# Expert products from raw 4-byte weights, with a branch on the token count

## The chip, the cores and the metric

One core of a Trainium2 chip runs the whole program. The metric is the device time of one execution in microseconds (us). Five engines work side by side: PE (TensorE: matrix products and, apart, the loads of their stationary operand), VectorE (DVE), ScalarE (ACT), GpSimd (POOL) and SyncE (SP, which issues most transfers). Products go to PSUM; operands lie in SBUF; DMA queues move data between SBUF and memory.

## The reference

One layer of a hybrid decoder on 1024 tokens of width 1024 in 4-byte floats: a modulated norm, one wide input projection, a recurrent branch, a sparse attention branch, a gated merge, and a mixture of 32 experts, of which each token uses two. Only the experts change:

```
xs = xf[row_tok].reshape(n_blk, MOE_BLOCK, D_)         # tokens of one expert, 128 to a block
hid = jax.nn.silu(xb @ w1[e]) * (xb @ w3[e])           # [128,1024] x [1024,512], twice
ys = hid @ w2[e]                                       # [128,512] x [512,1024]
out = segment_sum(ys * row_gate[:, None], row_tok)     # back to the tokens, then h += g2 * out
```

Counted from the reference's inputs, the 32 experts get 22 to 102 tokens: 17 of them at most 64, 11 from 65 to 96, 4 from 97 to 128, and none more.

## The kernel before

Everything up to the routing (the projections, attention, merge, output projection and the router's logits, in `project_out`) stays as it is but for a few lines at its end, where the lists of tokens and gates per expert are made. Then `experts` (L1395) runs over the 32 experts.

An expert has 128 slots, of which its tokens fill the first. Its weights, 6.29 MB, come as six transfers of 1 MB into a ring of 13 SBUF buffers (`ring_tile`, `prefetch`, `raw_load`: 8 buffers in `ring_a`, 5 in `ring_b`, which go back after expert 18). The transfers stand on SP's queue in the order in which they are used; each waits until its buffer is free.

PE multiplies in a rounded 4-byte format (`F32R`) in which each operand is the sum of a high and a low part. `weights` (L1464) splits each raw half buffer: ACT copies it to a rounded high part (L1472), VectorE subtracts that to get the low part (L1474). A product of two split operands is three products: high by high, high by low, low by high.

`expert` (L1458) is a generator that does one expert in steps:

- eight transposes on PE turn the 128 gathered token rows `xg` into `ptx` (L1483); ACT and VectorE split them into `xh` and `xl`;
- first products (L1501): the tokens stand still, 512 columns of w1 or w3 move; two sums `pa` and `pb` in PSUM over 8 blocks of 128 inputs, three products for each, so 48 in all;
- `hid` = silu(`pa`) x `pb` (L1506, L1507), four transposes into `pth` (L1483), and their split into `hh` and `hl`;
- last products (L137 to L139, `mm3`): `hid` stands still, 512 columns of w2 move; two sums `py`, 24 products;
- VectorE scales `py` by the gates and by the layer's gate row into `ye` (L1539), and POOL adds `ye` to the tokens' rows in memory by an indirect transfer (L1543). POOL also gathers the tokens of the expert that comes two later (L1453).

The loop in `experts` interleaves the steps, so that PE does the last products of expert e-1 beside the first of e and the transposes of e+1; within that, a scheduler sets the order on each engine. A branch (L1618) after expert 18 skips a loop for experts of more than 128 tokens, which these inputs don't need. The last two experts are not scattered: `combine` adds them by products with one-hot rows, makes the final norm and writes the output. Of what stands here, the change touches these functions:

Of the kernel before, what the change touches and what calls it, by code (L numbers as in the profile page):

```python
# [37 lines left out]
X_TAGS = [("xh", D), ("xl", D), ("hid", DE), ("hh", DE), ("hl", DE), ("ye", D)]  # L38
AHEAD = 3
NL = 4  # L40
RM = 4
RA, RB = 4 + RM, 5
NW = 6
RU = [-1, -1, -1, -1, -1, -1, -1, 6] + [3, 3, 4, 4, 4]
# [37 lines left out]
class Trunk:  # L82
# [866 lines left out]
    def merge(self, keep, ph):  # L949
# [21 lines left out]
        self.ring, self.uses = list(range(RA + RB)), list(RU)  # L971
# [164 lines left out]
    def project_out(self):  # L1136
# [5 lines left out]
        self.gate_l = hp.tile([P, NE], F32, name="gate_l")  # L1142
# [6 lines left out]
        with ExitStack() as st:  # L1149
# [128 lines left out]
            nc.scalar.activation(self.gate_l, R["gates"], AF.Copy)  # L1278
# [79 lines left out]
    def expert_weights(self, e, w1, w3, w2):  # L1358

        v1, v3 = (w.rearrange("(p k) f -> p (k f)", k=KT) for w in (w1, w3))  # L1360
        v2 = w2.rearrange("(p k) f -> p (k f)", k=4)
        h = [slice(0, 2048), slice(2048, 4096)]
        return [(v[:, h[c]], f"{n}_{e}_{c}") for c in range(2) for v, n in ((v1, "w1"), (v3, "w3"))] + [
            (v2[:, h[c]], f"w2_{e}_{c}") for c in range(2)
        ]

    def ring_tile(self, name, dt=F32):

        self.seq += 1
        i = self.ring.pop(0)  # L1370
        self.uses[i] -= 1
        if self.uses[i]:
            self.ring.append(i)
        pool, tag = (self.ring_a, f"ra{i}") if i < RA else (self.ring_b, f"rb{i - RA}")
        return pool.tile([P, 2048], dt, name=name, tag=tag)
# [19 lines left out]
    def experts(self):  # L1395

        nc, io = self.nc, self.io
        with ExitStack() as st:
# [4 lines left out]
            xp.tile([P, 640], F32, name="pad_at", tag="pad")  # L1403
            mp = self.pool(st, "moe")
            tp = self.pool(st, "moeps", bufs=2, space=PSUM)
            for n, b in (("whi", NW), ("wlo", NL)):
                mp.tile([P, D], F32R, name=f"{n}_at", tag=n, bufs=b)
# [6 lines left out]
            self.prefetch(RA + RB - self.seq)  # L1414
# [11 lines left out]
            def start(e):  # L1426
# [3 lines left out]
                if e < NE:  # L1430
                    gens[e] = self.expert(
                        xp, mp, tp, e, xgs[e % NXG], self.idx[:, e : e + 1], self.gate_l[:, e : e + 1],
                        [self.next_raw] * 6, NW, scatter=e < NE - 2,
                    )
                    step(e)
# [3 lines left out]
            for e in range(NE + 1):  # L1439
                step(e)  # L1440
                step(e - 1)
                step(e)
                start(e + 1)
                step(e - 1)
                if e == OV:

                    assert max(self.ring) < RA
                    rst.close()
                    self.overflow(xp, tp)
            self.combine(xp, mp, tp)  # L1450
# [7 lines left out]
    def expert(self, xp, mp, tp, e, xg, idx, gate, raws, nw, scatter=True):  # L1458
        nc = self.nc
        T = lambda n, e, shape, dt=F32: xp.tile(list(shape), dt, name=f"{n}_{e}", tag=n, bufs=2)  # L1460
        W = lambda n, e: mp.tile([P, D], F32R, name=f"{n}_{e}", tag=n, bufs=nw)
        raws = iter(raws)

        def weights(name):  # L1464
            raw = next(raws)()
            for g in range(2):
                hi, part = W("whi", f"{name}{g}"), raw[:, g * D : (g + 1) * D]
                lo = mp.tile([P, D], F32R, name=f"wlo_{name}{g}", tag="wlo", bufs=min(nw, NL))
                early = e == 0 and name[-1] == "0" and name[0] != "2"
                eng = nc.gpsimd if e == 0 and name[0] == "1" and name[-1] == "0" else nc.vector  # L1470
                with self.tc.issue_after(self.rooted) if early else nullcontext():
                    self.last_hi = nc.scalar.activation(hi, part, AF.Copy).ins  # L1472
                with self.tc.issue_after(self.listed) if early else nullcontext():
                    eng.tensor_tensor(lo, part, hi.bitcast(F32), op=OP.subtract)  # L1474
                yield hi, lo

        def tr(dst_h, dst_l, src, n, name):

            v = src.rearrange("t (p k) -> t k p", k=n)
            for g in range(0, n, 4):  # L1480
                pt = tp.tile([P, 4, P], F32, name=f"pt{name}_{e}_{g}", tag="pt")
                for k in range(4):
                    nc.tensor.transpose(pt[:, k, :], v[:, g + k, :], self.ident)  # L1483
                self.hilo(dst_h[:, g : g + 4, :], dst_l[:, g : g + 4, :], pt)

        xh, xl = T("xh", e, (P, KT, P), F32R), T("xl", e, (P, KT, P), F32R)
        tr(xh, xl, xg, KT, "x")
        yield
        pa = self.mmp.tile([P, 512], F32, name=f"pa_{e}", tag="mm")
        pb = self.mmp.tile([P, 512], F32, name=f"pb_{e}", tag="mm")  # L1490
        for c in range(2):
            if c:
                yield
            for ps, nm in ((pa, "1"), (pb, "3")):
                for g, (hi, lo) in enumerate(weights(f"{nm}_{e}_{c}")):

                    for b, As in ((hi, (xh, xl)), (lo, (xh,))):
                        for k in range(2):
                            kk = 4 * c + 2 * g + k
                            for a in As:  # L1500
                                nc.tensor.matmul(  # L1501
                                    ps, a[:, kk, :], b[:, k * DE : (k + 1) * DE], start=kk == 0 and a is xh and b is hi,
                                    stop=kk == KT - 1 and b is lo,
                                )
        hid = T("hid", e, (P, DE))
        nc.scalar.activation(hid, pa, AF.Silu)  # L1506
        nc.vector.tensor_tensor(hid, pb, hid, op=OP.mult)  # L1507
        yield
        hh, hl = T("hh", e, (P, 4, P), F32R), T("hl", e, (P, 4, P), F32R)
        tr(hh, hl, hid, 4, "h")  # L1510
        yield
        final = e == NE - 1
        pool, tag = (self.mmp, "mm") if final else (tp, "py")
        py = [pool.tile([P, 512], F32, name=f"py_{e}_{f}", tag=tag) for f in range(2)]

        def second(kk, f, hi, lo):
            s_ = slice(f * 512, (f + 1) * 512)
            self.mm3(py[f], hh[:, kk, :], hl[:, kk, :], hi[:, s_], lo[:, s_], kk == 0, kk == 3)

        for c in range(2):  # L1520
            w = weights(f"2_{e}_{c}")
            if final and c:
                w = list(w)
                for f in range(2):
                    for k in range(2):
                        second(2 + k, f, *w[k])
                continue
# [185 lines left out]
```

## Time and profile before

| | us |
|---|---|
| median of 3 runs (1865.74 to 1870.61) | 1866.28 |
| the profiled execution | 1865.06 |
| its span, first to last instruction | 1863.3 |
| PE busy | 1759.3 |
| VectorE busy | 1439.9 |
| ACT busy | 1170.1 |

The profile records every instruction with its start and a duration. Matmuls overlap: a matmul's duration covers filling and draining, so the time that PE spends on one is read from start to start. PEld is PE's loading of stationary operands, which overlaps PE. The granted clock is a share of 2.4 GHz: 1.00, or 0.50 for 1.2 GHz. "Idle before" is the time an engine stood still ahead of an instruction, with what ended it. Lines such as L1501 are lines of the kernel before.

### The profile page before, as it was taken

How to read it: one execution, taken by the hardware profiler on the slowest of the kernel's cores; microseconds unless marked ns; L12 is line 12 of the kernel's file. 1: busy time of each engine (PE TensorE's matmuls, PEld its weight loads, DVE VectorE, ACT ScalarE, POOL GpSimd, SP SyncE). 2: the span in 40 equal slices, each digit the busy share in tenths (PEclk: the TensorE clock that was granted, in tenths of full speed). 3: DMA queues.
4: the chain of work that ended last, by engine and by line, in shares of the span. 5: the costliest groups of instructions: out<-in, count | busy, mean ns of one | idle time of the engine just before them, and what ended most of it. 6: DMA issues, size and time to landing. Idle time of an engine off the chain costs nothing. (4 is left out here: it accounts for less than half of the span.)

```text
span 1863.3 us, 24597 instructions
## 1 busy us (share of the span) xinstructions
PE 1759.3 (94%) x8532; PEld 1456.1 (78%) x8532; DVE 1439.9 (77%) x2393; ACT 1170.1 (63%) x1730; POOL 398.8 (21%) x249
## 2 busy tenths in 40 slices
PE   3999999997999999999999999979999999999995
PEld 2788877786777888999788877858888888788774
DVE  6688876697777766778524456569999999999998
ACT  6565677725676767888512113348888887777765
POOL 4101002210010001212000001033554544344134
PEclk9999999998999999999999999979999999999998
DMA  9213754322112212121738544369989999999994
GB/s 297 61 35 104 237 179 147 109 89 65 59 54 73 68 58 93 55 66 57 216 107 252 194 152 170 138 238 350 379 329 344 363 376 367 366 380 371 357 338 182
DMA packets 163738, 366.85 MB, mean 197 GB/s; under 512 B 17855, under 2 KB 107543, under 8 KB 139160
## 3 DMA queue, kind: packets, MB, share of 16 engines
q1 hardware_dynamic: 152112, 340.50, 51.3%
q0 software_dynamic: 10192, 19.99, 3.9%
q10 hardware_dynamic: 1304, 4.74, 0.6%
q8 instruction: 68, 1.11, 0.3%
q14 instruction: 62, 0.51, 0.1%
HBM read 326.90 MB, written 54.53 MB: 205 GB/s over the span
## 5 line engine op out<-in xcount | busy, mean ns | idle before, releaser
L1472 ACT ACTIVATE whi<-raw_w 128x1024 fp32r<-128x1024 f32 x384 | 395.6, 1057 | 107.8 <-DMA raw_w<-in_moe_w_dram 28.2
L1474 DVE TENSOR_TENSOR wlo<-raw_w,whi 128x1024 fp32r<-128x1024 f32 x382 | 447.9, 1220 | 13.1 <-ACT whi L1472 4.7
L139 PE MATMUL pj<-uhi,wlo_in 128*128 128x512 f32 (+2 forms) x784 | 302.8, 387 | 5.6 <-POOL wlo_in L128 4.2
L137 PE MATMUL pj<-uhi,whi_in 128*128 128x512 f32 (+2 forms) x784 | 304.3, 388 | 1.2 <-ACT gq L706 1.2
L138 PE MATMUL pj<-ulo,whi_in 128*128 128x512 f32 (+2 forms) x784 | 302.0, 385 | 0.0
L1543 POOL DMA_INDIRECT h_spill<-ye,idx x30 | 179.4, 5980 | 215.0 <-DVE ye L1539 202.2
L139 PEld LDWEIGHTS pj<-uhi,wlo_in 128*128 128x128 f32 (+1 forms) x784 | 146.4, 187 | 37.8 <-POOL wlo_in L128 6.4
L137 PEld LDWEIGHTS pj<-uhi,whi_in 128*128 128x128 f32 (+1 forms) x784 | 146.6, 187 | 32.1 <-ACT gq L706 2.4
L138 PEld LDWEIGHTS pj<-ulo,whi_in 128*128 128x128 f32 (+1 forms) x784 | 146.6, 187 | 29.9 <-issue 1.0
L654 ACT ACTIVATE junk_a<-B,nt 128x768 bf16<-128x768 f32 (+2 forms) x93 | 96.8, 1041 | 49.6 <-DVE nt L650 41.2
L1501 PE MATMUL pa<-whi,xh 128*128 128x512 f32 x256 | 103.3, 403 | 0.6 <-ACT xh L97 0.5
L138 PE MATMUL py<-wlo,hh 128*128 128x512 f32 x256 | 100.9, 394 | 2.7 <-DVE wlo L1474 2.7
L1501 PE MATMUL pa<-whi,xl 128*128 128x512 f32 x256 | 100.6, 393 | 0.5 <-DVE xl L98 0.5
L137 PE MATMUL py<-gh,whi_y 128*128 128x512 f32 x256 | 99.9, 395 | 1.1 <-ACT gh L97 1.1
L1501 PE MATMUL pb<-whi,xh 128*128 128x512 f32 x256 | 100.0, 391 | 0.4 <-ACTq L1618 0.4
L139 PE MATMUL py<-gh,wlo_y 128*128 128x512 f32 x256 | 100.4, 393 | 0.0
L138 PE MATMUL py<-gl,whi_y 128*128 128x512 f32 x256 | 100.2, 393 | 0.1
L139 PE MATMUL py<-whi,hl 128*128 128x512 f32 x256 | 100.0, 391 | 0.0
L137 PE MATMUL py<-whi,hh 128*128 128x512 f32 x256 | 99.8, 400 | 0.1
L1501 PE MATMUL pb<-whi,xl 128*128 128x512 f32 x256 | 99.7, 389 | 0.0
L128 POOL TENSOR_TENSOR wlo_in<-raw_in,whi_in 128x1024 fp32r<-128x1024 f32 (+1 forms) x20 | 50.3, 2515 | 230.4 <-ACT whi_in L127 230.4
L127 ACT ACTIVATE whi_y<-raw_y 128x1024 fp32r<-128x1024 f32 x16 | 17.0, 1062 | 104.5 <-PE py L138 98.6
(403 smaller groups left out, 4119.2 us busy)
## 6 DMA issues: line engine op xcount, KB each, us to landing
raw_w<-in_moe_w_dram SPq DMA_DIRECT2D x191, 1024.0 KB, 12.6
raw_in<-in_w_in_dram SPq DMA_DIRECT2D x50, 512.0 KB, 3.5
wm<-in_w_mod_dram SPq DMA_DIRECT2D x32, 512.0 KB, 4.7
sg_spill<-gq SPq DMA_DIRECT2D x16, 512.0 KB, 2.6
sg<-sg_spill SPq DMA_DIRECT2D x32, 256.0 KB, 3.2
wm<-in_w_mod_dram SPq DMA_DIRECT2D x24, 256.0 KB, 5.8
g_spill<-ge SPq DMA_DIRECT2D x10, 512.0 KB, 2.6
gr<-g_spill SPq DMA_DIRECT2D x10, 512.0 KB, 3.6
```

What stands on the lines that cost most here:

```text
L127: nc.scalar.activation(hi[:, :n], raw[:, :n], AF.Copy)
L128: eng.tensor_tensor(lo[:, :n], raw[:, :n], hi[:, :n].bitcast(F32), op=OP.subtract)
L137: mm(ps, ah, bh, start=start, stop=False)
L138: mm(ps, ah, bl, start=False, stop=False)
L139: mm(ps, al, bh, start=False, stop=stop)
L654: nc.scalar.activation(junk_a[:, :n], self.B[j], AF.Sign, bias=nt[:, i : i + 1], accum_out=cnt[:, i : i + 1])
L1472: self.last_hi = nc.scalar.activation(hi, part, AF.Copy).ins
L1474: eng.tensor_tensor(lo, part, hi.bitcast(F32), op=OP.subtract)
L1501: nc.tensor.matmul(ps, a[:, kk, :], b[:, k * DE : (k + 1) * DE], start=kk == 0 and a is xh and b is hi, stop=kk == KT - 1 and b is lo,)
L1543: nc.gpsimd.indirect_dma_start(out=self.hd, out_offset=bass.IndirectOffsetOnAxis(ap=idx, axis=0), in_=ye, in_offset=None, bounds_check=S - ...
```

## The change

The weights are no longer split. In the first products the raw weights stand still, in blocks of 128 inputs by 128 hidden columns (every fourth column, so that the result is already turned for the last products), and the turned tokens move: 64, 96 or 128 slots, by the expert's count. PE reads the count into a register and branches; the other engines work on all 128 slots. Both sums take one PSUM bank each, `ph[0]` and `ph[1]`, and `hT` = silu(`ph[0]`) x `ph[1]` needs no transpose. In the last products 64 slots of `hT` stand still and 512 columns of the raw w2 move; the two halves of the output columns go to partitions 0 to 63 and 64 to 127 of one bank, `py[0]` for slots 0 to 63 and `py[1]` for the others, which is left out where the count is at most 64. All of these products are in plain 4-byte floats. The buffers of the split parts are gone; the ring gets 4 more (17 up to expert 18, 12 after it). PE's order is the one in which the loop writes it: `ptx` of e+1, last products of e-1, first products of e+1. The six transfers of an expert come in the order w1, w1, w3, w3, w2, w2.

```diff
-RA, RB = 4 + RM, 5
-NW = 6
+RA, RB, RC = 4 + RM, 5, 4
+RU = [-1] * RA + [5] * RB + [-1] * RC
...
+            nc.vector.tensor_copy(self.n_e, pn[:, :NE])
...
-            nc.scalar.activation(self.gate_l, R["gates"], AF.Copy)
+            for g in range(2):
+                self.both(self.gate_h[g], R["gates"][g * 64 : (g + 1) * 64, :])
...
+            self.ph = [tp.tile([P, 4, P], F32, name=f"ph_{i}") for i in range(2)]
+            self.py = [tp.tile([P, 512], F32, name=f"py_{i}") for i in range(2)]
...
+            for t in self.ph + self.py:
+                nc.vector.memset(t, 0.0)
...
-            for e in range(NE + 1):
-                step(e)
-                step(e - 1)
-                step(e)
-                start(e + 1)
-                step(e - 1)
+            for e0, e1 in ((0, OV + 1), (OV + 1, NE + 1)):
+                with self.as_traced((mybir.EngineType.PE,)):
+                    for e in range(e0, e1):
+                        step(e)
+                        start(e + 1)
+                        step(e - 1)
+                        step(e - 1)
...
+            n = nc.values_load(
+                count, engines=[mybir.EngineType.PE], min_val=0, max_val=S,
+            )
+        xT = T("xT", e, (P, KT, P))
...
+                nc.tensor.transpose(pt[:, k, :], v[:, g + k, :], self.ident)
+            nc.scalar.activation(xT[:, g : g + 4, :], pt, AF.Copy)
...
+        def first(m):
+            for ps, cs in zip(self.ph, w):
+                for b in range(4):
+                    for k in range(KT):
+                        blk = cs[k // 4][:, (k % 4) * DE : (k % 4 + 1) * DE].rearrange("p (f b) -> p b f", b=4)
+                        nc.tensor.matmul(
+                            ps[:, b, :m], blk[:, b, :], xT[:, k, :m], start=k == 0, stop=k == KT - 1
+                        )
...
+            with tc.If(n > 64) as more:
+                with tc.If(n > 96) as most:
+                    first(P)
+                with most.Else():
+                    first(96)
+            with more.Else():
+                first(64)
+        hid, hT = T("hid", e, (P, 4, P)), T("hT", e, (P, 4, P))
+        self.last_act = nc.scalar.activation(hid, self.ph[0], AF.Silu).ins
+        nc.vector.tensor_tensor(hT, self.ph[1], hid, op=OP.mult)
...
+        def second(g):
+            for k in range(4):
+                for f in range(2):
+                    nc.tensor.matmul(
+                        self.py[g][f * 64 : (f + 1) * 64, :], hT[:, k, g * 64 : (g + 1) * 64],
+                        w2[k // 2][:, (k % 2) * D + f * 512 : (k % 2) * D + (f + 1) * 512], start=k == 0, stop=k == 3,
+                    )
+        second(0)
...
+            with tc.If(n > 64):
+                second(1)
+        ye = T("ye", e, (P, D))
+        for g in range(2):
+            for f in range(2):
+                r, s_ = slice(f * 64, (f + 1) * 64), slice(f * 512, (f + 1) * 512)
+                nc.vector.scalar_tensor_tensor(
+                    ye[g * 64 : (g + 1) * 64, s_], self.py[g][r, :], gates[g][r, :], self.g2r[r, s_],
+                    op0=OP.mult, op1=OP.mult,
+                )
```

PE, from the token transposes that follow the first products of expert 1, in the kernel before (`whi` and `wlo` are split weights, the moving operand stands first):

```order
L1483 MATMUL ptx_0_11129<-ident,xg_10868 128x128 x4
L1483 MATMUL ptx_4_11136<-ident,xg_10868 128x128 x4
L137 MATMUL py_0_11143<-whi_0_00_11145,hh_11072 128x512
L138 MATMUL py_0_11143<-wlo_0_00_11146,hh_11072 128x512
L139 MATMUL py_0_11143<-whi_0_00_11145,hl_11073 128x512
...
L1501 MATMUL pa_11191<-whi_2_00_11193,xh_11127 128x512
L1501 MATMUL pa_11191<-whi_2_00_11193,xl_11128 128x512
...
L1483 MATMUL pth_0_11235<-ident,hid_11121 128x128 x4
```

And there after the change, with lines of the changed kernel (`raw_w` are unsplit weights; one row stands for matmuls on one buffer that follow each other):

```order
L1479 TENSOR_LOAD n_e
L1488 MATMUL ptx_0_11369<-ident,xg_10872 128x128 x4
L1488 MATMUL ptx_4_11375<-ident,xg_10872 128x128 x4
L1523 MATMUL py_10879<-raw_w_0_0_10902,hT_11142 64x512 x4
L1533 COMPARE_AND_BRANCH
L1523 MATMUL py_10880<-raw_w_0_0_10902,hT_11142 64x512 x4
L1506 COMPARE_AND_BRANCH
L1507 COMPARE_AND_BRANCH
L1499 MATMUL ph_10877<-xT_11368,raw_w_2_0_10906 128x128 x4
...
L1499 MATMUL ph_10877<-xT_11368,raw_w_2_0_10906 128x96 x4
...
L1499 MATMUL ph_10877<-xT_11368,raw_w_2_0_10906 128x64 x4
```

The register load and the branches are new, the hidden block's transposes are gone, and the first products stand there three times, of which one copy runs.

VectorE in about one expert's work before:

```order
L1539 SCALAR_TENSOR_TENSOR ye_11525<-py_1_11480,gate_l,modrow_3356 128x512
L1474 TENSOR_TENSOR wlo_4_01_11568<-raw_w_4_0_11555,whi_4_01_11567 128x1024
L1474 TENSOR_TENSOR wlo_4_10_11589<-raw_w_4_1_11586,whi_4_10_11588 128x1024
L98 TENSOR_TENSOR hl_11578<-pth_0_11579,hh_11577 128x512
L1474 TENSOR_TENSOR wlo_3_00_11657<-raw_w_3_0_11654,whi_3_00_11656 128x1024
L1507 TENSOR_TENSOR hid_11630<-pb_11532,hid_11630 128x512
L98 TENSOR_TENSOR xl_11637<-ptx_0_11638,xh_11636 128x512
```

and after:

```order
L1539 SCALAR_TENSOR_TENSOR ye_13162<-py_10880,gate_h_9612,modrow_3356 64x512
L1539 SCALAR_TENSOR_TENSOR ye_13162<-py_10879,gate_h_9611,modrow_3356 64x512
L1515 TENSOR_TENSOR hT_13119<-ph_10878,hid_13118 128x512
L1539 SCALAR_TENSOR_TENSOR ye_13162<-py_10879,gate_h_9611,modrow_3356 64x512
L1539 SCALAR_TENSOR_TENSOR ye_13162<-py_10880,gate_h_9612,modrow_3356 64x512
```

The twelve subtractions of an expert are gone, and with them the splits of tokens and hidden block; the scaling of the results is four instructions on 64 partitions instead of two on 128, two of them ahead of the next expert's multiply.

## Rows read from the trace of the kernel before

**Rows 1.** The page: busy time, share of the span and instructions of each engine.
```profile
PE 1759.3 (94%) x8532; PEld 1456.1 (78%) x8532; DVE 1439.9 (77%) x2393; ACT 1170.1 (63%) x1730; POOL 398.8 (21%) x249
```

**Rows 2.** Stretches of the experts' stage.
```profile
core 0: us, PE busy (x) PEld busy (x) DVE busy (x) ACT busy (x) POOL busy (x), PEclk, DMA share, GB/s
1300.00:1580.00 280.00, 280.00 (x1328) 234.83 (x1327) 274.66 (x283) 226.72 (x253) 136.09 (x32) 1.00 0.98 361
1248.08:1830.20 582.12, 575.87 (x2689) 477.17 (x2690) 555.53 (x569) 453.76 (x513) 241.21 (x68) 1.00 0.96 357
```

**Rows 3.** PE's waits in the experts' stage: total us, times, longest.
```profile
PE py L138 <- DVE wlo L1474: 2.7, 4, 0.9
PE ptx L1483 <- DMA xg<-n_spill,idx: 1.7, 1, 1.7
```

**Rows 4.** PE in order of time: start us, us, instruction.
```profile
1400.39 1.04 PE L1483 MATMUL ptx<-ident,xg 128*128 128x128 f32 x8
1401.51 0.39 PE L138 MATMUL py<-wlo,hh 128*128 128x512 f32 x1
1401.97 0.39 PE L137 MATMUL py<-whi,hh 128*128 128x512 f32 x1
1412.19 0.63 PE L1483 MATMUL pth<-ident,hid 128*128 128x128 f32 x4
1412.90 0.39 PE L1501 MATMUL pa<-whi,xl 128*128 128x512 f32 x1
```

**Rows 5.** PE's groups in one expert, 1400.39 to 1418.13 us: busy us, mean ns.
```profile
L1501 PE MATMUL pa<-whi,xh 128*128 128x512 f32 x8 | 3.2, 401 | 0.0
```

**Rows 6.** PE's groups of the whole program: the router's logits.
```profile
L1227 PE MATMUL plog<-wr,hT 128*128 128x40 f32 x128 | 16.0, 276 | 0.0
```

**Rows 7.** PE in order of time: the logits of one token tile.
```profile
1129.74 1.03 PE L1227 MATMUL plog<-wr,hT 128*128 128x40 f32 x8
1130.60 0.63 PE L1212 MATMUL put<-ident,h 128*128 128x128 f32 x4
1131.31 0.39 PE L139 MATMUL pout<-woh,ml 128*128 128x512 f32 x1
```

**Rows 8.** PE in order of time: plain 4-byte products of 512 columns.
```profile
222.83 1.88 PE L1092 MATMUL pm<-macc,ones 128*128 128x512 f32 x4
224.78 0.40 PE L138 MATMUL pj<-ulo,whi_in 128*128 128x512 f32 x1
```

**Rows 9.** PE's sequencer: the branch after expert 18, ns.
```profile
L1618 PEldq COMPARE_BRANCH  x1: 450/450/450, 1582.0 to 1582.0; - x1
```

**Rows 10.** PE in order of time, behind that branch.
```profile
1584.05 0.39 PE L139 MATMUL py<-whi,hl 128*128 128x512 f32 x1
1584.59 0.47 PE L1501 MATMUL pa<-whi,xh 128*128 128x512 f32 x1
```

**Rows 11.** The page's queue of instructions: packets, MB, share of 16 DMA engines.
```profile
q8 instruction: 68, 1.11, 0.3%
```

**Rows 12.** ACT's and VectorE's groups in one expert, 1400.39 to 1418.13 us.
```profile
L1472 ACT ACTIVATE whi<-raw_w 128x1024 fp32r<-128x1024 f32 x13 | 13.7, 1060 | 3.5 <-PE pb L1501 1.0 <-PE py L139 0.9 <-ACT xh L97 0.8
...
L1474 DVE TENSOR_TENSOR wlo<-raw_w,whi 128x1024 fp32r<-128x1024 f32 x13 | 15.2, 1216 | 0.2
L1539 DVE SCALAR_TENSOR_TENSOR ye<-py,gate_l,modrow 128x512 f32<-128x512 f32 x2 | 1.4, 740 | 0.0
L1507 DVE TENSOR_TENSOR hid<-pb,hid 128x512 f32<-128x512 f32 x1 | 0.7, 693 | 0.2 <-PE pb L1501 0.2
```

**Rows 13.** DMA from 1300 to 1580 us: total, then a queue's packets, MB, share.
```profile
DMA packets 17196, 101.14 MB, mean 361 GB/s; under 512 B 3815, under 2 KB 3815, under 8 KB 5910
q0 software_dynamic: 4504, 8.59, 12.3%
```

**Rows 14.** Stretches with few moved columns; the granted clock is PEclk.
```profile
1244.47:1246.20 1.73, 1.73 (x8) 1.73 (x8) 1.73 (x2) 0.00 (x0) 1.43 (x2) 0.50 0.28 45
1227.84:1229.80 1.96, 1.96 (x19) 1.88 (x18) 1.87 (x6) 1.96 (x6) 1.27 (x1) 1.00 0.84 341
```

More of the change, by code (lines that the diff above doesn't have):

```diff
@@ L1456, in gather @@
         )
[L1458 to L1487, printed above, removed]
-        yield
[L1489 to L1507, printed above, removed]
-        yield
-        hh, hl = T("hh", e, (P, 4, P), F32R), T("hl", e, (P, 4, P), F32R)
-        tr(hh, hl, hid, 4, "h")
-        yield
[L1512 to L1527, printed above, removed]
-            for k, (hi, lo) in enumerate(w):
-                for f in range(2):
-                    second(2 * c + k, f, hi, lo)
-        ye = T("ye", e, (P, D))
-        for f in range(2):
-            s_ = slice(f * 512, (f + 1) * 512)
-            if e == NE - 2:
-                nc.scalar.activation(ye[:, s_], py[f], AF.Copy, scale=gate)
-                nc.gpsimd.tensor_tensor(ye[:, s_], ye[:, s_], self.g2r[:, s_], op=OP.mult)
-            else:
-                nc.vector.scalar_tensor_tensor(ye[:, s_], py[f], gate, self.g2r[:, s_], op0=OP.mult, op1=OP.mult)
@@ new lines, in expert @@
+    def expert(self, xp, e, xg, idx, gates, raws, count=None, scatter=True):
+        nc, tc = self.nc, self.tc
+        T = lambda n, e, shape: xp.tile(list(shape), F32, name=f"{n}_{e}", tag=n, bufs=2)
+        n = None
+        if count is not None:
+            n = nc.values_load(
+                count, engines=[mybir.EngineType.PE], min_val=0, max_val=S,
+                skip_runtime_bounds_check_because="a token counts once",
+            )
+        xT = T("xT", e, (P, KT, P))
+        v = xg.rearrange("t (p k) -> t k p", k=KT)
+        for g in range(0, KT, 4):
+            pt = self.mmp.tile([P, 4, P], F32, name=f"ptx_{e}_{g}", tag="mm")
+            for k in range(4):
+                nc.tensor.transpose(pt[:, k, :], v[:, g + k, :], self.ident)
+            nc.scalar.activation(xT[:, g : g + 4, :], pt, AF.Copy)
+        yield
+        w = [[next(raws_)() for _ in range(2)] for raws_ in [iter(raws[:2]), iter(raws[2:4])]]
+        def first(m):
[6 more added lines that the diff above has]
+                        )
+        if n is None:
+            first(P)
+        else:
+            with tc.If(n > 64) as more:
+                with tc.If(n > 96) as most:
+                    first(P)
+                with most.Else():
[5 more added lines that the diff above has]
+        nc.vector.tensor_tensor(hT, self.ph[1], hid, op=OP.mult)
+        yield
+        w2 = [raws[4 + c]() for c in range(2)]
+        def second(g):
+            for k in range(4):
+                for f in range(2):
[4 more added lines that the diff above has]
+        second(0)
+        yield
+        if n is None:
+            second(1)
+        else:
+            with tc.If(n > 64):
+                second(1)
+        ye = T("ye", e, (P, D))
+        for g in range(2):
+            for f in range(2):
+                r, s_ = slice(f * 64, (f + 1) * 64), slice(f * 512, (f + 1) * 512)
+                nc.vector.scalar_tensor_tensor(
+                    ye[g * 64 : (g + 1) * 64, s_], self.py[g][r, :], gates[g][r, :], self.g2r[r, s_],
+                    op0=OP.mult, op1=OP.mult,
+                )
@@ L1564, in combine @@
         nc.vector.tensor_copy(ix, self.idx[:, NE - 2 : NE])
[L1565 removed]
+        y = [self.ring_tile(f"fin_y{i}", F32R).rearrange("p (z d) -> p z d", d=D) for i in range(2)]
+        y = [(v[:, 0, :], v[:, 1, :]) for v in y]
         for i in range(2):
```

69 lines of the change are left out of this document (36 added, 33 removed).

## The prediction

> **What bounds the kernel now.** I read the busy times first. PE is busy 94% of the span, and VectorE 77% [rows 1]. Then the stages: from 1248.08 us, where the first token block is turned, to 1830.20 us the 32 experts run, 582.1 us in all, and inside it PE, VectorE and the DMA are all near full: in 1300 to 1580 us PE is busy throughout, VectorE 274.66 of 280 us, the DMA share is 0.98 [rows 2]. So which of them sets the pace? The list of PE's waits in that stage answers it: PE waited 5.5 us in six entries (the largest 2.7) for other engines in 582 us, and once for the gathered tokens [rows 3]. PE sets the pace; the other two are just fast enough.
>
> What PE's pace is made of is read from starts, since the matmuls overlap and their mean of 401 ns [rows 5] is no interval. Between 1401.51 and 1401.97 us two products of 512 columns start, 0.23 us each; over a whole expert it is 0.2275. From 1400.39 to 1401.51 stand eight transposes of the token block and one product: (1.12 - 0.2275)/8 = 0.1116 us each. From 1412.19 to 1412.90 four transposes of the hidden block and one product: (0.71 - 0.2275)/4 = 0.1206 us [rows 4]. An expert has 72 products (9 groups of 8, of which one stands in [rows 5]), 8 and 4 transposes: 72 x 0.2275 + 8 x 0.1116 + 4 x 0.1206 = 16.38 + 0.89 + 0.48 = 17.75 us, the period (1400.39 to 1418.13), and 32 x 17.75 = 568. The other 14 us are waits and a slow clock at its start.
>
> **The change part by part.**
>
> First products. Before: 48 products, 10.92 us. After: 2 matrices x 4 blocks x 8 = 64 products in plain 4-byte floats. The trace has such products: the router's logits, 8 token tiles x 8 in the code, stand in it as 128 matmuls, each with a weight load of its own [rows 6]. A plain 4-byte product is thus two matmuls and two loads of 128 columns. Their interval, with only 40 columns moved: from 1129.74 to 1131.31 us stand eight of them, four transposes and one product, so (1.57 - 0.2275 - 4 x 0.1116)/8 = 0.112 us [rows 7]. Moving 40 columns is not what takes that long: 512 columns of the same kind take (224.78 - 222.83 - 0.2275)/4 = 0.43 us [rows 8], 0.84 ns a column, so 40 columns take 0.034, 64 take 0.054, 96 take 0.081 and 128 take 0.108. The weight load sets the 0.112, and it stays the longer of the two at 64 and 96 moved columns and level at 128. So the count changes almost nothing in the first products; 128 matmuls per expert remain whatever branch is taken. The new loads step through the raw weights by 4 floats; the transposes of the hidden block load with that same step and take 0.1206, those of the tokens, with a step of 8, take 0.1116 [rows 4]. Bounds: 128 x 0.112 = 14.3 and 128 x 0.1206 = 15.4 us; the logits are the nearest row in kind and the hidden block in step, so I take the middle, 14.9. That is +3.98 x 32 = +127 us (109 to 144).
>
> Hidden transposes: four per expert go, -0.48 x 32 = -15 us. The token transposes stay.
>
> Last products. Before: 24 x 0.2275 = 5.46, x 32 = 175 us. After: a half of 64 slots is 8 products of 512 plain columns, or 16 matmuls. Counted from the reference's inputs, 17 experts have at most 64 tokens and need one half, 15 need both: 47 halves. The two products that follow each other in a half write different 64 partitions, from 64 stationary columns each, so the second can run beside the first; the two matmuls of one product can't. In order of issue that is 8 x 0.43 + 0.43 = 3.87 us a half, 182 us, +7. No row shows two column halves at work at once. The bounds: at the pace of the split floats (one 512-column stream in 0.2275) 16 x 0.2275 = 3.64, 171 us, -4; one after the other 16 x 0.43 = 6.88, 323 us, +148. I take 3.87, since nothing in the order makes the second wait; the upper end is a rival below. The Trainium skill, TensorEngine Tiling (Array Packing), Available Configurations and Key Properties, has 128 rows by 64 columns as two tiles that load and multiply independently, and lets a change of mode drain the engine first; by that rule the +7 stands, and no row here can confirm it.
>
> Branches. Each expert gets a register load and two to four branches on PE. The trace has one branch on PE, at L1618: it took 0.45 us on the sequencer, hidden behind queued products, and PE lost 0.31 us (0.54 from start to start, less 0.2275) to an emptied queue [rows 9, 10]. For the 17 small experts the skipped half first waits until PE is done, so nothing is queued and both show: 0.76 x 17 = 13 us, the lower end. For the upper end: the jumps pass one or two blocks of 256 matmul and load instructions. Instructions arrive in packets of 1.11 MB / 68 = 16.3 KB, each 0.3% x 16 x 1863 / 68 = 1.3 us long [rows 11]. Two such fetches on top, 3.4 us for the 17 and 1 us for the others, make 73 us. I take 30, nearer the one branch that the trace shows. The Trainium skill, Runtime: NRT & Kernel Launch, Instruction fetch mechanics, speaks against the change: a taken branch out of the two pages at hand waits for a fetch. By the rule 21 jumps over two blocks cost 1.3 us each, which with the 13 is 40; without it the 13 stand alone.
>
> What leaves ACT and VectorE: 12 splits of 1.06 us and 12 of 1.22 us per expert [rows 12]. Neither was the pace, so it gives back only PE's waits for them, -5 us (0 to -14, the whole excess of the stage). What stays: VectorE 0.69 + 4 x 0.74 = 3.7 us per expert, ACT three operations of that size, beside 19 us or more of PE. VectorE holds two scalings of expert e-1 ahead of the multiply of e, but the first group of e+1 covers that with 7 us. If that cover went, up to 3.7 us per expert would show.
>
> DMA. Bytes and queue stay. At 361 GB/s [rows 13] an expert's 6.29 MB of weights and 8.59/16 = 0.54 MB of gather and scatter take 18.9 us, under the new period of 19.7 to 23.5: hidden, by little. Four more buffers help no rate. The memsets and copies at the end of routing, at most 4 x 0.69 us on VectorE, stand beside the gather that PE waits for: 0 (to +3).
>
> **Sum.** 127 - 15 + 7 + 30 - 5 = +144. The profiled execution took 1865.06 us (span 1863.3), 0.07% under the median of 1866.28, so 2009 us. Low ends: 109 - 15 - 4 + 13 - 14 = +89, 1954; high ends without the serial halves: 144 - 15 + 7 + 73 + 3 = +212, 2077. In periods: 14.9 + 0.9 + 3.9 = 19.7 us for a small expert and 23.5 for one over 64, before branches.
>
> **Rivals.**
> 1. The halves run one after the other: 323 instead of 182 us, 2150 us (2095 to 2218). For it: every 4-byte row of the trace is serial [rows 8]. Against it: the halves share neither stationary columns nor output partitions.
> 2. Faster. If a weight load hid behind any matmul, the first products would take what they stream: 128 x 0.054, 0.081 or 0.108, or 6.9, 10.3 and 13.8 us for 17, 11 and 4 experts, 286 us; with 182 and the 29 of token transposes 497 us of PE. Then the DMA ends last: 17 buffers are filled ahead (2.8 experts), 29.2 x 18.9 = 552 us against 582, so 1835 us. It decides only from a period under 18.2 us, where 32 periods make the old stage. Against it stands the 0.112 us at 40 columns [rows 7]. The same would follow from a count that mattered.
> 3. The clock falls in the first products of small experts, where 64 columns move behind each weight load. At a granted clock of 0.50 eight matmuls on 32 columns took 1.73 us, 0.216 each, twice the 0.112 [rows 14]; PE had mostly stood idle before. For 17 experts: 17 x 128 x (0.216 - 0.1165) = +217, 2226 us. Against it: from 1227.84 us sixteen matmuls of the logits ran, among others, with the clock at 1.00 [rows 14], though briefly.
>
> **Chances.** The forecast 0.64, rival 1 0.19, rival 2 0.07, rival 3 0.08, the rest (time near the old one) 0.02. The range from 1952 to 2165 holds the forecast with its bounds and more than half of rival 1; the two that it leaves out are mostly rivals 2 and 3 and the top of 1. Runs of this kernel tell 0.3% from no change. Faster 0.07, within it 0.02, slower 0.91.
>
> **What would show it.** Right: 128 matmuls with 128 weight loads in the first products of each expert, at 0.11 to 0.12 us from start to start with 64 as with 128 columns; in the last products two starts close together and a half in about 3.9 us; an expert's period 4 us longer above 64 tokens; ACT and VectorE under a third busy; no wait for weights. Wrong: first products of an expert of 64 near 7 us (rival 2), 6.9 us a half (1), a granted clock of 0.5 inside the stage (3), or gaps of over 3 us on PE after the branches.

## The result, and the profile after

The changed kernel takes 2570.23 us (median of 4 runs, 2568.69 to 2572.04) against 1867.47 us for the kernel before on the same chip: a ratio of 1.376, with a 95% interval of 1.374 to 1.379. Slower was forecast, but the time lies 405 us above the top of the range, above every rival too. The profiled execution took 2569.19 us; its span is 2567.2.

The page's busy times, where [rows 1] stood:

```profile
PE 2393.0 (93%) x10948; PEld 2044.4 (80%) x10948; DVE 992.9 (39%) x1986; ACT 769.0 (30%) x1315; POOL 239.0 (9%) x245
```

The stretches of [rows 2], the second from the first token transpose to the last of the last products:

```profile
1300.00:1580.00 280.00, 277.60 (x1186) 243.59 (x1186) 25.56 (x35) 11.56 (x21) 18.32 (x14) 0.62 0.53 174
1255.20:2532.30 1277.10, 1204.02 (x5105) 1061.06 (x5105) 112.57 (x156) 57.43 (x101) 85.48 (x63) 0.65 0.49 163
```

PE still fills the stage, which has grown from 582.1 to 1277.1 us. VectorE went from 274.66 to 25.56 us of the same 280, the DMA share from 0.98 to 0.53: what the change takes from them is not what was paid for. Two things are new: the granted clock is 0.62 instead of 1.00, and PE's loads of weights are busy nearly as long as PE.

PE in order of time (start us, us, instruction), to be set against [rows 4]; first an expert of 128 columns, then one of 64:

```profile
1634.24 1.04 PE L1488 MATMUL ptx<-ident,xg 128*128 128x128 f32 x8
...
1639.42 30.11 PE L1499 MATMUL ph<-xT,raw_w 128*128 128x128 f32 x128 [0.56 <-PEq L1533]
1669.46 1.13 PE L1488 MATMUL ptx<-ident,xg 128*128 128x128 f32 x8
1670.52 7.09 PE L1523 MATMUL py<-raw_w,hT 128*64 128x512 f32 x32
1677.54 30.13 PE L1499 MATMUL ph<-xT,raw_w 128*128 128x64 f32 x128
1707.46 1.91 PE L1488 MATMUL ptx<-ident,xg 128*128 128x128 f32 x8
1709.30 7.85 PE L1523 MATMUL py<-raw_w,hT 128*64 128x512 f32 x32
```

There are the 128 matmuls per expert that were forecast, and the count indeed changes nothing: 30.04 us with 128 columns, 29.92 with 64. But that is 0.234 us from start to start, twice the 0.1165 of the sum. And the clock does not set it. Here are the same two experts as stretches (columns as above: the last three are granted clock, DMA share, GB/s):

```profile
1639.42:1669.40 29.98, 29.98 (x128) 29.92 (x128) 3.18 (x5) 0.00 (x0) 1.58 (x1) 1.00 0.49 169
1677.54:1707.40 29.86, 29.86 (x130) 29.86 (x129) 3.60 (x5) 0.00 (x0) 1.58 (x1) 0.60 0.51 156
```

The first ran at 1.00 and the second mostly at 0.50 (0.60 in the mean), in the same time. The token transposes behind them do show the clock: eight in 1.06 us (1669.46 to 1670.52) or in 1.84 (1707.46 to 1709.30). The last products do as well: two halves in 7.02 us at the full clock (1670.52 to 1677.54), 3.51 a half where 3.87 was forecast.

PE's waits in the stage, beside [rows 3] ("issue" is time in which the profile shows nothing that PE waited for):

```profile
PE ph L1499 <- issue: 65.3, 17, 12.0
PE ptx L1488 <- DMA xg<-n_spill,idx: 10.9, 1, 10.9
PE ph L1499 <- PEq L1533: 4.7, 6, 1.0
```

The 65.3 us are PE's own branches. Its sequencer (count: least/median/longest ns), for the test against 64, the one against 96 and the end of its paths, and the test ahead of the second half; [rows 9] had one branch of 450 ns:

```profile
L1506 PEldq COMPARE_BRANCH  x32: 65/3310/4957, 1255.8 to 2484.5; - x32
L1507 PEldq COMPARE_BRANCH  x30: 65/346/7118, 1256.0 to 2512.3; - x30
L1533 PEldq COMPARE_BRANCH  x47: 65/183/353, 1325.6 to 2528.0; - x47
```

The branch over the few instructions of one half takes 0.07 to 0.35 us. The one at L1506 takes 0.07 in the 15 experts that fall through; in the 17 in which it skips the 512 matmul and load instructions of the 128- and 96-column copies it takes 3.3 to 5.0. The trace shows what these wait for: each of the 23 PE branches of over 2.5 us in the stage has a whole packet of the instruction queue [rows 11] inside it, and none of the 84 under 0.6 us has one. Behind a small expert nothing is queued on PE, and such a jump shows in full.

### The profile page after: what moved, and what is told of

It is laid out like the page before. It is cut to its first block, busy times and chain, and to the rows that moved or that the text cites. A ratio compares the mean times of both kernels' runs of the same rounds, so it can differ in the third digit from the quotient of the medians.

```text
span 2567.2 us, 27984 instructions
## 1 busy us (share of the span) xinstructions
PE 2393.0 (93%) x10948; PEld 2044.4 (80%) x10948; DVE 992.9 (39%) x1986; ACT 769.0 (30%) x1315; POOL 239.0 (9%) x245
## 5 line engine op out<-in xcount | busy, mean ns | idle before, releaser
L1499 PEld LDWEIGHTS ph<-xT,raw_w 128*128 128x128 f32 x4096 | 958.5, 329 | 95.6 <-issue 95.4
L1499 PE MATMUL ph<-xT,raw_w 128*128 128x64 f32 (+2 forms) x4096 | 964.7, 431 | 70.0 <-issue 65.3
L1539 DVE SCALAR_TENSOR_TENSOR ye<-py,gate_h,modrow 64x512 f32<-64x512 f32 x128 | 96.0, 750 | 1129.2 <-PEq L1533 610.6
L1489 ACT ACTIVATE xT<-ptx 128x512 f32<-128x512 f32 x64 | 37.6, 597 | 1180.9 <-PE ptx L1488 1180.8
L1523 PE MATMUL py<-raw_w,hT 128*64 128x512 f32 x752 | 191.7, 663 | 0.0
L1523 PEld LDWEIGHTS py<-raw_w,hT 128*64 128x64 f32 x752 | 56.7, 156 | 115.6 <-issue 114.9
L1546 POOL DMA_INDIRECT h_spill<-ye,idx x30 | 47.4, 1581 | 336.7 <-DVE ye L1539 336.7
L618 DVE TENSOR_SCALAR_CACHE_REDUCE junk<-B,trial 128x384 bf16<-128x384 f32 (+2 forms) x93 | 69.1, 744 | 1.9
L125 ACT ACTIVATE whi_in<-raw_in 128x1024 fp32r<-128x1024 f32 (+1 forms) x51 | 53.3, 1045 | 46.1 <-PE pj L136 41.1
L1488 PE MATMUL ptx<-ident,xg 128*128 128x128 f32 x256 | 56.6, 395 | 10.9 <-DMA xg<-n_spill,idx 10.9
```

Of the source, the lines that this page charges most:

```text
L125: nc.scalar.activation(hi[:, :n], raw[:, :n], AF.Copy)
L618: nc.vector.tensor_scalar(junk[:, :n] if dst is None else dst, src, thr_ap, 0.0, op0=op, op1=OP.add, accum_out=out,)
L1499: nc.tensor.matmul(ps[:, b, :m], blk[:, b, :], xT[:, k, :m], start=k == 0, stop=k == KT - 1)
L1523: nc.tensor.matmul(self.py[g][f * 64 : (f + 1) * 64, :], hT[:, k, g * 64 : (g + 1) * 64], w2[k // 2][:, (k % 2) * D + f * 512 : (k % 2) * ...
L1539: nc.vector.scalar_tensor_tensor(ye[g * 64 : (g + 1) * 64, s_], self.py[g][r, :], gates[g][r, :], self.g2r[r, s_], op0=OP.mult, op1=OP.mult,)
L1546: nc.gpsimd.indirect_dma_start(out=self.hd, out_offset=bass.IndirectOffsetOnAxis(ap=idx, axis=0), in_=ye, in_offset=None, bounds_check=S - ...
```

## The experiments

The question was first what a load of 0.233 us is made of, then what the clock and the branches cost by themselves.

**Step 1.** Blocks of 128 columns that lie side by side, and w2's rows loaded to fit:

```diff
-v2 = w2.rearrange("(p k) f -> p (k f)", k=4)
+v2 = w2.rearrange("(k p) f -> p k f", k=4)
...
-blk = cs[k // 4][:, (k % 4) * DE : (k % 4 + 1) * DE].rearrange("p (f b) -> p b f", b=4)
+c0 = (k % 4) * DE + b * P
...
-    ps[:, b, :m], blk[:, b, :], xT[:, k, :m], start=k == 0, stop=k == KT - 1
+    ps[:, b, :m], cs[k // 4][:, c0 : c0 + P], xT[:, k, :m], start=k == 0, stop=k == KT - 1
```

> The changed kernel with weight blocks of 128 columns that lie side by side (step 1) instead of every fourth; w2 is loaded in the row order that fits. Theory A, the step of 4 floats sets the 0.233 us of a weight load: with step 1 a load takes what the logits took, 0.112 us at a granted clock of 1.00 and 0.213 at 0.50. If the clock holds, the first products fall from 30.0 to 14.3 us an expert, 32 x 15.6 = 500 us, and the time to about 2070 us, or some 40 us less if the transposes and last products also run at the full clock. If the clock stays at 0.50, 27.3 us an expert, and about 2480 us. Theory B, plain 4-byte weights that come fresh from memory cost 0.233 us a load in any order (their buffers, the PSUM banks or the short moves are the reason): unchanged, 2540 to 2600 us.

Measured: 2256.78 us (2241.80 to 2263.64, 4 runs), ratio 1.208 (1.202 to 1.213). PE in order of time, two experts of 64 columns:

```profile
1461.07 14.51 PE L1506 MATMUL ph<-xT,raw_w 128*128 128x64 f32 x128
1475.41 1.09 PE L1495 MATMUL ptx<-ident,xg 128*128 128x128 f32 x8
...
1569.30 25.04 PE L1506 MATMUL ph<-xT,raw_w 128*128 128x64 f32 x128 [0.59 <-issue]
1594.13 1.91 PE L1495 MATMUL ptx<-ident,xg 128*128 128x128 f32 x8
```

and their stretches:

```profile
1461.07:1475.40 14.33, 14.33 (x130) 14.33 (x129) 3.59 (x5) 0.00 (x0) 1.58 (x1) 1.00 0.91 292
1569.30:1594.10 24.80, 24.80 (x128) 24.80 (x129) 3.05 (x5) 0.00 (x0) 1.58 (x1) 0.56 0.57 181
```

At the full clock 14.34 us, 0.112 a load, as the logits of [rows 7] had it; at half clock 0.213 (the median of the loads that ran at 0.50). So the step set the 0.233 (theory A), and theory B fell. The time lies between A's two cases because the clock did not hold: counted over all starts, 70% of the 64-column loads came 0.21 us apart, 6% of the 96-column and 3% of the 128-column ones.

**Other steps.** By turns, an expert takes its weight columns with step 2, with step 8, as 2-byte numbers 16 bytes apart, or with step 1; other columns than the reference's enter the products, and only the intervals are read:

```diff
+elif e % 4 == 0:
+    blk = c[:, q * DE + b // 2 * 256 :][:, :256].rearrange("p (f b) -> p b f", b=2)[:, b % 2, :]
+elif e % 4 == 1:
+    blk = c[:, q // 2 * 1024 :][:, :1024].rearrange("p (f b) -> p b f", b=8)[:, q % 2 * 4 + b, :]
...
```

> The first products of every fourth expert take their weight columns by another step: step 2, step 8, the upper halves of every fourth float as 2-byte numbers (one record instead of two per product, 16 bytes from column to column), and step 1; other columns of the weights enter the products than in the reference. What is read are the intervals in the trace. Theory A with a line of 16 bytes as its unit: step 1 and step 2 at 0.112 us (0.213 at half clock), step 8 at 0.233 like step 4, and the 2-byte load with 16 bytes from column to column slow as well. Theory A with a cost that grows with the distance: step 2 between 0.112 and 0.233, step 8 near 0.45. Theory A2, only the two-record loads of plain 4-byte products suffer (the transposes, one record each, loaded with steps of 4 and 8 floats in 0.12 and 0.11): the 2-byte load is fast, 0.12 us or less. Theory B: 0.233 in all the 4-byte forms.

PE in order of time; step 2, step 8, 2 bytes and step 1, all of 96 columns:

```profile
1369.18 15.30 PE L1512 MATMUL ph<-xT,raw_w 128*128 128x96 f32 x128 [0.83 <-PEq L1544]
1384.31 1.07 PE L1488 MATMUL ptx<-ident,xg 128*128 128x128 f32 x8
...
1396.17 30.34 PE L1512 MATMUL ph<-xT,raw_w 128*128 128x96 f32 x126 [5.61 <-issue]
1426.31 1.56 PE L1488 MATMUL ptx<-ident,xg 128*128 128x128 f32 x8
...
1434.82 4.37 PE L1512 MATMUL ph<-xT,raw_w 128*128 128x96 bf16 x64
1439.03 1.12 PE L1488 MATMUL ptx<-ident,xg 128*128 128x128 f32 x8
...
1447.09 14.53 PE L1512 MATMUL ph<-xT,raw_w 128*128 128x96 f32 x128
```

From start to start: step 2 (1384.31 - 1369.18)/128 = 0.118 us, step 8 (1426.31 - 1396.17)/126 = 0.239, hardly more than step 4. Step 1 took 0.112 in the median. So the cost does not grow with the distance: it comes once, between 8 and 16 bytes from column to column. The 2-byte load at 16 bytes took (1439.03 - 1434.82)/64 = 0.066 with its first waits, 0.061 in the middle, and 0.060 where the clock stood at 0.50. By the expectation so fast a load speaks for theory A2 and not for the line of 16 bytes; the next run decides that. The Trainium skill, SBUF — State Buffer, Specifications (TRN2), says that SBUF has lines of 16 bytes and gives its full bandwidth where a line is hit at least twice. The 4-byte rows agree: two columns a line cost 0.118, one column a line 0.233. The 2-byte row can't settle it, since no run has a 2-byte load without a step to compare. That lines are the reason is thus a fit to the 4-byte rows.

**One record or two.** The rounded format, one record per product, from one fixed block of zeros instead of the weights, with steps 1, 2, 4, 8 by turns (the ring has one buffer fewer):

```diff
+s = 1 << (0 if e == "ov" else e % 4)
+blk = self.rw[:, : P * s].rearrange("p (f s) -> p s f", s=s)[:, b % s, :]
...
```

> The first products in the rounded 4-byte format, one record each, from one fixed stationary block (zeros, not the weights) with steps of 1, 2, 4 and 8 floats by turns of the experts. If only two-record loads suffer from the step: 0.112 to 0.12 us at all four steps at the full clock (as the transposes, 0.11 and 0.12 at steps of 8 and 4). If every 4-byte load outside a transpose does: 0.23 at steps 4 and 8.

PE in order of time:

```profile
1455.34 7.93 PE L1502 MATMUL ph<-xT,rw 128*128 128x128 f32 x64
1463.11 1.13 PE L1490 MATMUL ptx<-ident,xg 128*128 128x128 f32 x8
...
1468.27 15.19 PE L1502 MATMUL ph<-xT,rw 128*128 128x128 f32 x64 [0.45 <-PEq L1536]
1483.26 1.93 PE L1490 MATMUL ptx<-ident,xg 128*128 128x128 f32 x8
```

Step 2: 7.77/64 = 0.121 us (median 0.118); step 4: 14.99/64 = 0.234. One record suffers as two do: theory A2, that only plain 4-byte products are hit, fell. Then why did the transposes of [rows 4], with steps of 8 and 4, take 0.11 and 0.12?

**What a transpose loads.** Step 1, no branches; in odd experts the unit matrix has a step of 4 (the ring has one buffer fewer):

```diff
-nc.tensor.transpose(pt[:, k, :], v[:, g + k, :], self.ident)
+nc.tensor.transpose(pt[:, k, :], v[:, g + k, :], self.wide if e != "ov" and e % 2 else self.ident)
```

> The step-1 kernel without branches, and in the token transposes of every odd expert the unit matrix lies with a step of 4 floats; the tokens' rows have their step of 8 in all of them. If the tokens' rows are what a transpose loads (as the prediction took it from the program's operands), a load with a step of 8 floats can cost 0.11 us, and the unit matrix only moves: 0.11 us for all transposes, and why they are spared stays open. If a transpose loads the unit matrix and moves the rows: 0.233 us in the odd experts, 0.11 in the even ones, and then the two rows of before on which the 0.1206 rested showed no strided load at all.

PE in order of time, an odd and an even expert (`wide` is the unit matrix with the step):

```profile
1354.37 2.00 PE L1499 MATMUL ptx<-wide,xg 128*128 128x128 f32 x8
1356.30 7.09 PE L1534 MATMUL py<-raw_w,hT 128*64 128x512 f32 x32
...
1377.71 1.04 PE L1499 MATMUL ptx<-ident,xg 128*128 128x128 f32 x8
1378.68 2.80 PE L1534 MATMUL py<-raw_w,hT 128*64 128x512 f32 x12
```

1.93 against 0.97 us for eight; the median interval is 0.23 against 0.11, what a stepped and an unstepped load cost in the runs above. The whole run took 2021.94 us (one run), 14 more than the step-1 kernel without branches further down; 16 odd experts at 0.96 make 15. So what a transpose loads is the unit matrix, and the tokens' rows move, with a step of 8 floats at no visible cost. The other reading, in which the rows are loaded and the moving unit matrix is slowed by its step, was not tried by itself; it would need a load with a step of 8 to take 0.11 in a transpose and 0.239 in a product. The rows from which the stepped load was priced thus showed no stepped load.

**No branch.** Step 4 as in the change, 128 columns and both halves for all:

```diff
-if count is not None:
+if False:
```

> The changed kernel without the count and the branches: every expert does its first products with 128 slots and both halves of the last. First products: the load sets the interval at 64, 96 and 128 columns, so 30.0 us an expert as before. The gaps ahead of the first products (62 us in all in the trace of the changed kernel) and 10 us inside them go; 17 more halves come, at 3.5 us each at the full clock (+60) and up to 7 at half (+119). So 2560 to 2620 us if branches cost what their gaps show. If the branches cost nothing beyond work hidden anyway: 2630 to 2690. If the count did matter in the first products, they would grow for 17 experts and show intervals above 0.233.

Measured: 2503.85 us (one run), 66 us less, with 17 halves more work and below the expected 2560 to 2620. The stretch of [rows 2]:

```profile
1300.00:1580.00 280.00, 280.00 (x1238) 245.50 (x1239) 25.83 (x35) 12.38 (x22) 18.32 (x14) 1.00 0.54 180
```

PE has no gap and the clock is 1.00. What I had left out is that the clock comes back: the transposes took 29 us in all instead of 51, and each half 3.51. Branches and small counts went together here, so this run can't tell which of them had held the clock down.

**Step 1, branches and clock apart.** Three variants of the step-1 kernel: without any branch; with all branches, but 128 columns in each path; and with 128 columns and only the branch ahead of the second half.

```diff
# no branch
-if count is not None:
+if False:
# all 128: in the two other paths
-first(96)
+first(P)
...
-first(64)
+first(P)
# last branch only: the three paths behind `else:` are not taken
-if n is None:
+if True:
     first(P)
```

> Weight blocks with step 1, no count and no branches, 128 slots and both halves for every expert. If the sum of the prediction was right but for the load, an expert takes 128 x 0.112 = 14.3, two halves of 3.51, eight transposes 0.97: 22.3 us, 32 of them 714 us, and with the 1283 us of the rest about 2000 us. If the clock falls in these first products as it did with 64 columns in the step-1 kernel (0.213 us a load), up to 2400 us.

> The step-1 kernel with all its branches, but each of the three paths moves 128 columns. Theory C, the granted clock falls where only 64 columns move per load (0.213 us in 70% of those loads, in 6% at 96 and 3.5% at 128): the loads of all experts go back to 0.112, and the time to 1283 + 32 x 14.4 + 29 + 47 x 3.51 + 80 of gaps after branches = 2020 us (1990 to 2060), although more columns move. Rival, the stops of PE at the branches make the clock fall: near the 2257 us of the step-1 kernel.

> The step-1 kernel with 128 columns and no branch in the first products; the branch on the second half of the last products stays. If the long gaps (3 to 7 us) come from the jumps over 256 or 512 instructions of the first products, only the short ones stay, about 1 us for each of the 17 experts that skip a half: 1283 + 32 x 14.3 + 31 + 165 + 17 = 1955 us. If a branch costs the same wherever it jumps, some 40 us more, 1995.

Measured: 2007.55 us (one run), 2104.66 (one run) and 1967.34 (4 runs, 1963.12 to 1969.28; ratio 1.054, 1.051 to 1.057). The no-branch kernel in order of time:

```profile
1420.05 1.04 PE L1495 MATMUL ptx<-ident,xg 128*128 128x128 f32 x8
...
1428.04 14.56 PE L1506 MATMUL ph<-xT,raw_w 128*128 128x128 f32 x128
1442.43 1.04 PE L1495 MATMUL ptx<-ident,xg 128*128 128x128 f32 x8
```

An expert in 22.38 us (1420.05 to 1442.43), as expected, 14.39 of it the first products. More moved columns made the all-128 kernel 152 us faster than the step-1 kernel: its clock over the span is 0.960 instead of 0.889, which bears out theory C more than its rival; but it missed the expected 1990 to 2060. Still 7% of its loads came 0.21 us apart, against 1% in the two others, so the branches hold the clock down a little as well. PE's waits in the all-128 kernel,

```profile
PE ph L1506 <- issue: 80.6, 25, 11.5
PE ptx L1495 <- issue: 21.3, 9, 7.4
```

and in the one with the last branch only:

```profile
PE ph L1506 <- issue: 4.1, 1, 4.1
PE ph L1506 <- PEq L1540: 3.5, 11, 0.4
```

The branches around the first products cost 2104.7 - 1967.3 = 137 us. The stops come to 102 us in the one and 8 in the other; most of the rest goes with the clock, 0.960 over the span against 0.982 (492 us against 463 for the first products without their stops). PE waited for the branch over half an expert's last products 11 times, 0.3 us each, and that branch saves 40 us against no branch at all. The time of 1967.34 lies nearer the first case of its expectation (1955) than the second (1995).

**Order of the halves.** The last products written half by half instead of in pairs:

```diff
-for k in range(4):
-    for f in range(2):
+for f in range(2):
+    for k in range(4):
```

> The changed kernel with the last products written by output half first (four blocks of inputs for the left half, then four for the right), so that matmuls of different column halves no longer follow each other but once in eight. Theory: two halves run side by side only when their matmuls are neighbours in PE's order; then a half of 64 slots takes 16 x 0.43 = 6.9 us instead of 3.5 at the full clock, 47 x 3.4 = +160 us, 2700 to 2800 us. Rival: PE takes any later matmul of the other half ahead, and the order does not matter: 2570 us.

Measured: 2625.49 us (one run), +55, between the two expectations. PE in order of time:

```profile
1487.04 8.97 PE L1523 MATMUL py<-raw_w,hT 128*64 128x512 f32 x32
1495.94 1.41 PE L1499 MATMUL ph<-xT,raw_w 128*128 128x96 f32 x5
```

8.90 us for two halves: 4.45 each, where pairs took 3.51 and matmuls one by one would take 6.9. So halves run side by side, best as neighbours, and PE finds part of the overlap itself.

**Tokens standing still.** The runs pointed to a version without stepped loads and with pairs everywhere: 64 tokens stand, w1 moves into the lower and w3 into the upper partitions.

```diff
+def first(g):
+    for k in range(KT):
+        for f, cs in enumerate(w):
+            nc.tensor.matmul(
+                ph[g][f * 64 : (f + 1) * 64, :], xT[:, k, g * 64 : (g + 1) * 64],
+                cs[k // 4][:, (k % 4) * DE : (k % 4 + 1) * DE], start=k == 0, stop=k == KT - 1,
+            )
...
+first(0)
...
+    with tc.If(n > 64):
+        first(1)
```

> The tokens stand still again, 64 slots at a time in plain 4-byte floats: w1 moves past them into partitions 0 to 63 and w3 at the same time into 64 to 127, 512 columns each; the hidden block is transposed as in the kernel before; the second 64 slots stand behind a branch in the first and in the last products. No weight load is waited for, 512 columns move per load, so the clock should hold. If two column halves run side by side here as in the last products: 8 x 2 x 0.43 = 6.9 us a half in the first products, 3.5 in the last, 0.97 and 0.48 for transposes: 11.8 us for the 17 small experts and 22.3 for the others, 535 us, and with 1 us for each of 34 skipped halves 569: 1850 us (1835, where the transfers end last, to 1900). If the halves don't overlap: 17 x 22 + 15 x 43, 2300 us.

Measured: 1891.44 us (4 runs, 1888.90 to 1894.41), ratio 1.014 (1.012 to 1.017). A large and a small expert:

```profile
1449.89 13.95 PE L1499 MATMUL ph<-raw_w,xT 128*64 128x512 f32 x64
1463.78 1.16 PE L1488 MATMUL ptx<-ident,xg 128*128 128x128 f32 x8
1464.86 7.09 PE L1527 MATMUL py<-raw_w,hT 128*64 128x512 f32 x32
1471.88 0.74 PE L1518 MATMUL pth<-ident,hid 128*128 128x128 f32 x4
1472.56 7.09 PE L1499 MATMUL ph<-raw_w,xT 128*64 128x512 f32 x32
1480.36 1.13 PE L1488 MATMUL ptx<-ident,xg 128*128 128x128 f32 x8 [0.72 <-PEq L1508]
```

The first products take 13.9 us for two halves and 7.0 for one, and the clock over the span is 0.976. The time lies above the expected 1850 but within its 1835 to 1900; it is near the kernel before and not under it. One more run asked whether the stop at the branch for large counts was to blame:

```diff
-RU = [-1] * RA + [5] * RB + [-1] * RC
+RU = [-1] * RA + [10] * RB + [-1] * RC
-OV = 18
+OV = 29
```

> The tokens-still kernel with the branch for experts of more than 128 tokens after expert 29 instead of 18, and the five buffers of the second ring used until then. In the tokens-still kernel PE stood 5.7 us at that branch, and in the eight small experts behind it 13 us for weights that came late; behind expert 29 all weights are on their way. If that is what kept it above the kernel before: 1891 - 6 - 13 to 22 = 1863 to 1872 us, within 0.4% of the kernel before (1865), since 17 x 13.33 + 15 x 22.66 = 567 us of PE against 568. If the transfers themselves can't follow the row of small experts (13.3 us each against 18.9 us a transfer of an expert's weights, with 17 buffers ahead): 1880 to 1890.

Measured: 1886.70 us (5 runs, 1882.34 to 1888.97), ratio 1.011 (1.009 to 1.014): its second case. The stop stays, only later, and weights still come late. PE's waits:

```profile
PE ptx L1488 <- PEq L1508: 12.2, 17, 0.8
PE ph L1499 <- DMA raw_w<-in_moe_w_dram: 8.9, 3, 4.4
PE ph L1499 <- DVEq L1626: 5.4, 1, 5.4
```

The late weights come between 1665 and 1706 us, in the last two of a row of nine small experts and in the one behind them, and there the transfers are at their most. DMA from 1640 to 1720 us, beside the 361 GB/s of [rows 13]:

```profile
DMA packets 5281, 30.49 MB, mean 381 GB/s; under 512 B 1312, under 2 KB 1312, under 8 KB 1817
```

No version that was run beats the kernel before.

## Why the prediction was wrong

The profiled execution is 2569.2 - 2009 = 560 us over the forecast. By terms, from PE's starts in the stage:

| term, 32 experts | forecast us | measured us | difference |
|---|---|---|---|
| first products | 477 | 964 | +487 |
| token transposes | 29 | 51 | +22 |
| last products | 182 | 186 | +4 |
| branches, between PE's groups | 30 | 72 | +42 |
| the rest of the program and small stalls | | | +5 |

- **The step that failed** is the price of a load in the first products: "the transposes of the hidden block load with that same step and take 0.1206". They load the unit matrix, as the run with the stepped unit matrix shows. The rows at hand held a warning: in [rows 7] four transposes of rows without any step come out at (1131.31 - 1130.60 - 0.2275)/4 = 0.1206 us too, so that figure was no price of a step. I had read which operand stands from the order in which the program lists them, and the logits, the nearest row in kind, have no step. So both bounds, 0.112 and 0.1206, were prices without a step, and the upper end was no upper end. The mechanism, 128 loads that set the pace whatever the count, was right: with step 1 and the full clock the first products take 14.39 us an expert (14.9 forecast). That the step-1 kernel without branches takes 2007.55 us, near the 2009 forecast, is partly chance: its loads come to 462 us (-15), its 64 halves to 225 (+43), and the branches (-30) are gone.
- **Rival 3** (the clock) was true as a mechanism and nearly free here. The clock in the stage is 0.65, but a stepped load takes 0.233 us at either level, so the fall shows only in transposes and last products, +22 and +21 us. Nor was it only the small experts: in their first products those of 64 and of 96 columns ran at 0.50 to 0.60 in the mean, and the four of 128 at 0.95 to 1.00. With step 1 the clock does cost: 152 us between the step-1 kernel and the one that always moves 128 columns, where 217 were threatened. I gave it 0.08, on the strength of 2 us of logits at 1.00 [rows 14].
- **Rival 1** fell: the two matmuls of a pair of column halves start 7 ns apart in the records, and a half takes 3.51 us. At the full clock 47 halves would take 165 us, even below the lower bound of 171; the fall of the clock brought them to 186, so the nearness to the 182 forecast is luck.
- **Rival 2** fell: in the first products no load hid behind a matmul, and the DMA share is 0.53.
- **Branches** were taken at 30 us with bounds of 13 and 73; the gaps between PE's groups are 72. The one branch of [rows 9, 10] was a short one with a queue behind it and no instruction packet in it. The fetches in the upper bound are what the long ones show, but longer: a packet took 0.97 us (the 1.3 came from a rounded share), a jump that waited for one 3.3 to 5.0 at L1506. In the run with one record per product, whose copies are half as long, only 2 of the 110 branches took over 2.5 us. The rule cited from the Trainium skill, Runtime: NRT & Kernel Launch, Instruction fetch mechanics, that a jump out of the pages at hand waits for a fetch, agrees with a packet in every long branch and none in a short one. Where such a jump stood right behind the branch for large counts, one gap was 12.0 us.
- **Gather.** The first token block waited 10.9 us for its gather, against 1.7 before [rows 3]; the few operations at the end of routing, costed at 0 to 3 us, are the likeliest reason, which was not tried.
- **ACT, VectorE, DMA** behaved as forecast: all far under the pace in the stage, and no wait of PE for weights.

## What to carry to other kernels

Price a weight load by a row that has the same operand standing and the same step; check which operand stands by a run or by a row in which only one of them has a step, not from the order of arguments. Lay 4-byte weights so that the columns of a block lie side by side or two floats apart: at a step of 4, a block of 128 costs 0.233 us instead of 0.112 (at 8, 0.239), and no clock brings it back. Before work is skipped by a branch, set what it saves against the fetch behind the jump and against the clock in the stage: here, with step 1, moving 128 columns always, with one short branch left, was 289 us faster than moving just what was needed.

## What the hardware showed that I had not expected

- A stepped load of 128 columns takes 0.233 us (step 4) and 0.239 (step 8) at a granted clock of 1.00 as of 0.50, while loads at steps 1 and 2 go from 0.112 and 0.118 to 0.213.
- A moving operand with a step of 8 floats costs nothing visible: eight transposes in 0.97 us.
- A jump of PE that waits for instructions shows in the trace: every PE branch of over 2.5 us (23 in the changed kernel, 31 in the all-128 one) has a whole packet of the instruction queue in it, no branch under 0.6 us has one.
- Doing more can be faster: with step 1, 2104.66 us with 128 columns in every path (one run), 2256.78 with the counts.
- Column halves overlap in part (4.45 us) even where eight matmuls of one half stand ahead of the other.
